# One copy per attention unit moved from VectorE to ScalarE, and sixteen subtractions moved from GpSimd to VectorE, in a float32 decoder layer

## The chip, the core and the metric

The kernel runs on one core of a Trainium2 chip. A core has five engines that run side by side, each through its own instructions in their written order: TensorE (PE in the profile, with its weight loads as PEld), VectorE (DVE), ScalarE (ACT), GpSimd (POOL) and SyncE (SP), which here issues most DMAs. An engine that comes to an instruction whose input is not ready stands still, with everything behind it. The metric is the device time of one execution in microseconds (us).

## The reference, cut to what matters

One decoder layer on 2048 tokens of width 1024, all in float32:

```
mod = silu(c) @ w_ada + b_ada ;  shift, scale, gate = split(mod)
u = x * (1 + scale) + shift
q, k, v, a_gate, p_in, p_gate, m_a, m_p = split(u @ w_in)
a = sliding_window_attention(q, k, v, sinks, bias) * silu(a_gate)  -> @ w_attn_proj
p = causal means of p_in over 2, 4, 8, 16 tokens, minus p_in, by quarter of the width
p = (grouped(p) * pool_scale) * silu(p_gate)                       -> @ w_pool_proj
y = (sigmoid(m_a) * a + sigmoid(m_p) * p) @ w_out * (1 + gate)
out = layer_norm(alpha * x + y)
```

Attention has 16 query heads on 2 key and value heads of 64, a window of 128 tokens, a bias by distance and one extra "sink" logit per head.

## The kernel before, in words

**Exact products from a faster format.** TensorE multiplies in a format that keeps fewer bits than float32 (`F32R`). So each operand is split into a high part (a copy with that type, by ScalarE) and a low part (the operand minus the high part, helper `low`, line 130), and each product is three matmuls: high by high, high by low, low by high (`mm3`). A split of a weight block therefore costs one ScalarE copy and one subtraction, both of 128x512. The split pair stands in a buffer `w_set`, of which there are four.

**Quads.** Dense products are done four at a time. A quad takes two column tiles of weights and two halves of 512 tokens, and gets its four results from seven block products instead of eight, with sums and differences of blocks formed beforehand. The seven are named by their block: T2, B21, T3, B22, B11, T4, T1. Each is 12 matmuls of 128x512 (four slices of the contraction, three matmuls each). The weight sums are made in place in a buffer `W` by GpSimd: `sum1`, then `mid` (two subtractions, which give the blocks of T2 and T3), then `late`. Between the block products VectorE and ScalarE combine accumulators: after T2, for instance, VectorE adds `b = c + p5` (written `mm<-mm,p` in the profile), and T3 may not start before that, since T3 goes on adding into `c`.

**Stages.** The tokens are done in two halves of 1024. Each half has a stage of plain quads (gates, keys, values) and then an attention stage (function `attention`, line 746). After both halves come the output projections and the norm. The change lies inside `attention` alone, which runs twice: from about 270 to 618 us and from about 846 to 1197 us of the profile.

**The attention stage.** It interleaves two streams. The first are 64 units, one per block of 128 queries and pair of heads, and a loop over `n` in which pass `n` works on several units at once. On TensorE a pass is: scores of unit n (`lg<-kk,qs`), transposes of the probabilities of unit n-2 (`pt<-ident,L`), a share of the second stream, and the value product of unit n-2 (`pv<-pth,vv` and `pv<-ptl,vv`). On VectorE: reciprocal of the sums of unit n-1 (`sm`), the treatment of the value product of unit n-3 (line 988 and the two adds behind it), scores plus bias and row maximum (the two `CUSTOM` instructions), the low part of the transposed probabilities (`ptl`), and the scaling of the second head's probabilities (`TENSOR_SCALAR L<-L,sm`). On ScalarE: the scaling of the first head's probabilities (`L<-L,sm`), the high part of the transposed probabilities (`pth`), and two exponentials (`L<-L,nm`).

The value matrix holds high and low part side by side, so a value product comes out as 128 rows: 64 rows from the high part and 64 from the low part. VectorE copies the lower 64 rows from the accumulator to a tile `o2` (`o<-pv`, 64x256) and then adds them to the upper 64 in two adds. This copy is line 988.

The second stream are 13 quads called fills: products for the next steps that fill TensorE's time between a unit's dependent steps. Their order is mix 0, ma 0, q 2, mix 2, ma 2, q 4, mix 4, ma 4, mp 0, q 6, mix 6, ma 6, mp 2, numbered x = 0 to 12. The four "mix" quads end in the pooled branch: GpSimd sums each result over 2, 4, 8 or 16 tokens in doubling steps (`nxt<-vb`, `nxt<-nxt`, `fin<-nxt`), VectorE scales it and subtracts (`fin<-fin,...`), GpSimd multiplies it with its gate (`fin<-fin,pg`). Mix 4 (x = 6) pools over 8 tokens and mix 6 (x = 10) over 16. "q" quads end in the split of queries (`qs`) by ScalarE and VectorE.

The weight split of a block product is written three block products ahead of its use (`split`, line 860): a high part by ScalarE, then a low part by GpSimd, except for the blocks T1, whose low part VectorE makes:

```
            act.copy(hi, q.block(name))
            low(dve if name == "T1" else pool, lo, q.block(name), hi)
            if name == "T1":
                q.mid(pool)
```

So `mid` of a quad stands on GpSimd behind everything written before it, and the high part of T2 on ScalarE waits for `mid`. The order of all these instructions on each engine is the written order; no planner moves them inside the stage.

Of the kernel before, what the change touches and what calls it, by code (L numbers as in the profile page):

```python
# [27 lines left out]
HD = 64  # L28
# [6 lines left out]
POOL_W = (2, 4, 8, 16)  # L35
# [24 lines left out]
def kernel(  # L60
# [23 lines left out]
    pe, act, dve, pool, sp = (Ordered(tc, e) for e in (nc.tensor, nc.scalar, nc.vector, nc.gpsimd, nc.sync))  # L84
# [42 lines left out]
    def as32(ap):  # L127
        return ap.bitcast(F32)

    def low(engine, dst, src, hi):  # L130
        engine.tensor_tensor(dst, src, as32(hi), ALU.subtract)  # L131
# [614 lines left out]
    def attention(ph, s, fills, post, opened):  # L746
# [5 lines left out]
        def ld(name, src, bufs):  # L752
            x = tp.tile([P, CH], F32, tag=name, bufs=bufs, name=name)
            sp.dma_start(x, src)
            return x
# [99 lines left out]
        for i in range(len(seq)):  # L855
            lead = 2 if seq[i] == (K + 1, "B11") else 3
            splits.setdefault(i - lead, []).append(i)
        made, st = {}, {0: [*opened[0][:2], None, None]}

        def split(i):  # L860
            x, name = seq[i]
            q = quads[x]
            if name == "B11" and x > 1:
                q.sum1(pool)
            w = ph.split()
            hi, lo = made[i] = w[:, 0:CH], w[:, CH:]
            act.copy(hi, q.block(name))
            low(dve if name == "T1" else pool, lo, q.block(name), hi)
            if name == "T1":
                q.mid(pool)  # L870
            elif name == "B21":
                q.late(pool)

        def begun(i):
            x, name = seq[i]
            if name == "T1":
                st[x][1] = bank()
                if x < K:
                    later(free_b[0], lambda: seed(x))
                    if free_b[0] < now_n[0]:  # L880
                        run_coming()
            if name == "B11":
                st[x] = [bank(), None, None, None]
                if x < K:
                    quads[x + 1].load(ph, False, sp, None)
            if (x, name) == (K - 1, "B22"):
                quads[K + 1].load(ph, False, sp, None)
            for j in splits.get(i, ()):
                split(j)
# [71 lines left out]
        for i in range(-3, 0):  # L961
            for j in splits.get(i, ()):
                split(j)
# [4 lines left out]
        for n in range(N + 3):  # L968
# [11 lines left out]
            if n - 3 in pvs:  # L980
                pv = pvs.pop(n - 3)
                jj, tt, bb = (n - 3) // U, (n - 3) // NB % 2, (n - 3) % NB
                if bb == 0:
                    outs[jj, tt] = tp.tile([P, CH], F32, tag="o", bufs=2, name="o")
                if bb == 1:
                    ags[jj, tt] = ld("ag", gates_d["ag"][s, jj, tt], 1)
                o2 = tp.tile([HD, 2, P], F32, tag="o2", bufs=1, name="o2")
                dve.tensor_copy(o2, pv[HD:])
                for h in range(2):
                    dve.tensor_tensor(  # L990
                        outs[jj, tt][h * HD : (h + 1) * HD, bb * P : (bb + 1) * P], pv[0:HD, h, :], o2[:, h, :], ALU.add
                    )
# [461 lines left out]
    with Pools("a0") as ph:  # L1454
        opened = attention(ph, 0, plans[0][1], plans[0][2], opened)
# [4 lines left out]
    with Pools("a1") as ph:  # L1460
        opened = attention(ph, 1, plans[1][1], plans[1][2], opened)
# [96 lines left out]
```

## Time and profile before

| what | us |
|---|---|
| median of 3 runs (lowest, highest) | 1728.08 (1727.62, 1729.83) |
| the profiled execution | 1731.03 |
| its span, first to last instruction | 1729.2 |
| busy over the span: PE, DVE, POOL, ACT | 1664.1, 1254.5, 1058.1, 964.2 |
| busy in the first attention stage (348.0): PE, DVE, POOL, ACT | 342.9, 264.2, 260.0, 238.8 |
| busy in the second (351.0): PE, DVE, POOL, ACT | 346.4, 267.3, 259.7, 244.1 |

The profiled execution is 2.95 us slower than the median of the runs, and 1.83 us longer than its span. A row of a timeline reads: start, duration, engine, line, operation, output<-inputs, shape and count, and in brackets the idle time of the engine before it and what ended that wait. Ends of matmuls are modelled, so gaps on TensorE are better read from start to start.

### The profile page before, as it was taken

To read this page: it belongs to the slowest core of one execution; us is meant where nothing else is said; L and a number is where in the kernel's file an instruction comes from. 1 tells how busy PE (TensorE), PEld (TensorE's weight loads), DVE (VectorE), ACT (ScalarE), POOL (GpSimd) and SP (SyncE) were. 2 spreads that over 40 slices of the span, in tenths; PEclk is the share of its full clock that TensorE was granted. 3 is DMA by queue.
4 is the path that set the end of the run, shared out by engine and by line. 5 is a ranking of instruction groups with operands and counts; after the bars stand their busy time and mean duration, and the time that the engine had idled before them with its cause. 6 is when DMAs were issued, how large, how long until landed. Compare 5 with 4: busy or idle time off the path is not lost.

```text
span 1729.2 us, 24722 instructions
## 1 busy us (share of the span) xinstructions
PE 1664.1 (96%) x8056; PEld 1392.5 (81%) x8056; DVE 1254.5 (73%) x2256; ACT 964.2 (56%) x2002; POOL 1058.1 (61%) x782
## 2 busy tenths in 40 slices
PE   6899999999999999999999999999999989999996
PEld 5788888888888788887788888888787767787885
DVE  5966665787778768557578777786778576868877
ACT  4544446667667655334667676765644345434452
POOL 2054427686867837763476778594657875666442
PEclk9999999999999999999999999999999989999999
DMA  9388753333432377866533434235987887787442
GB/s 353 131 283 287 218 188 111 117 108 122 149 107 95 129 250 277 282 226 207 188 110 104 132 118 153 86 116 185 326 294 275 310 305 272 263 274 239 158 139 105
DMA packets 188849, 336.79 MB, mean 195 GB/s; under 512 B 18336, under 2 KB 44080, under 8 KB 188720
## 3 DMA queue, kind: packets, MB, share of 16 engines
q1 hardware_dynamic: 185600, 330.96, 55.7%
q10 hardware_dynamic: 3088, 4.23, 1.0%
q8 instruction: 64, 1.05, 0.3%
q14 instruction: 65, 0.53, 0.1%
q0 software_dynamic: 32, 0.02, 0.0%
HBM read 227.96 MB, written 110.33 MB: 196 GB/s over the span
## 4 chain that ended last, share of the span: by engine, by line
PE 47%; POOL 7%; DVE 5%; DMA 4%; issue 4%; ACT 1%; SPq 0%; POOLq 0%; DVEq 0%; ACTq 0%
PE mm L56 30%; PE lg L56 13%; PE pv L56 2%; PE pt L56 2%; DVE w_set L131 1%; POOL spare L56 1%; POOL nxt L56 1%; POOL W L268 1%; POOL w_set L56 1%; POOL fin L56 1%; DMA W<-in_wpp_dram 1%; DMA W<-in_wap_dram 1%; DMA pin_T<-spare 1%; POOL wide L612 1%; DVE set_T L56 1%
## 5 line engine op out<-in xcount | busy, mean ns | idle before, releaser
L56 PE MATMUL mm<-set_B,w_set 128*128 128x512 f32 x2664 | 664.8, 397 | 18.3 <-ACT w_set L305 10.5
L56 PEld LDWEIGHTS mm<-set_B,w_set 128*128 128x128 f32 x2664 | 501.2, 190 | 129.1 <-ACT w_set L305 12.6
L56 PE MATMUL mm<-set_T,w_set 128*128 128x512 f32 x1824 | 457.4, 397 | 3.8 <-DVE mm L56 1.2
L56 PE MATMUL lg<-set_T,w_set 128*128 128x512 f32 x1728 | 417.9, 392 | 10.0 <-DVE w_set L131 4.8
L56 PEld LDWEIGHTS mm<-set_T,w_set 128*128 128x128 f32 x1824 | 337.7, 189 | 76.4 <-DVE mm L56 4.1
L56 PEld LDWEIGHTS lg<-set_T,w_set 128*128 128x128 f32 x1728 | 323.9, 189 | 82.7 <-DVE w_set L131 8.4
L131 DVE TENSOR_TENSOR w_set<-W,w_set 128x1024 fp32r<-128x1024 f32 x138 | 198.4, 1439 | 185.9 <-ACT w_set L305 172.8
L305 ACT CAST w_set<-W 128x1024 fp32r<-128x1024 f32 x138 | 144.8, 1050 | 291.0 <-PE mm L56 164.4
L56 POOL TENSOR_TENSOR w_set<-W,w_set 128x512 fp32r<-128x512 f32 x132 | 172.0, 1311 | 102.5 <-ACT w_set L56 98.1
L268 POOL TENSOR_TENSOR W<-W,A 128x512 f32<-128x512 f32 x46 | 70.6, 1535 | 223.8 <-DVE set_T L56 58.2
L56 ACT ACTIVATE L<-L,nm 128x257 f32<-128x257 f32 (+1 forms) x256 | 127.1, 498 | 26.0 <-DVE nm L56 20.2
L56 POOL TENSOR_TENSOR W<-W 128x512 f32<-128x512 f32 x82 | 108.3, 1335 | 51.1 <-DVE sm L56 30.3
L277 POOL TENSOR_TENSOR W<-W 128x512 f32<-128x512 f32 x46 | 72.8, 1583 | 101.6 <-DVE w_set L131 94.0
L56 DVE CUSTOM_DVE_ANT_0 L<-lg,bt,nsink 128x256 f32<-128x256 f32 (+1 forms) x256 | 111.6, 473 | 19.0 <-DMA bt<-e_rep 9.1
L56 POOL TENSOR_TENSOR spare<-spare 128x512 f32<-128x512 f32 x68 | 117.2, 1725 | 12.6 <-DMA spare<-ain_B 8.7
L56 ACT CAST w_set<-W 128x512 fp32r<-128x512 f32 (+1 forms) x164 | 100.0, 626 | 37.4 <-POOL W L56 25.8
L56 DVE COPY o<-pv 64x256 f32<-64x256 f32 x128 | 54.3, 424 | 82.7 <-PE pv L56 81.4
L56 ACT CAST pth<-pt 128x512 fp32r<-128x512 f32 (+1 forms) x128 | 72.8, 569 | 62.8 <-PE pt L56 62.4
L56 ACT ACTIVATE L<-L,sm 128x256 f32<-128x256 f32 (+1 forms) x128 | 64.3, 502 | 67.9 <-DVE sm L56 67.7
L272 POOL TENSOR_TENSOR W<-W 128x512 f32<-128x512 f32 x44 | 75.6, 1720 | 39.1 <-DVE w_set L131 30.1
L273 POOL TENSOR_TENSOR W<-W 128x512 f32<-128x512 f32 x44 | 77.5, 1761 | 28.3 <-DMA W<-in_win_dram 26.6
L56 DVE TENSOR_SCALAR L<-L,sm 128x256 f32<-128x256 f32 (+1 forms) x128 | 89.8, 701 | 0.0
(225 smaller groups left out, 2474.8 us busy)
## 6 DMA issues: line engine op xcount, KB each, us to landing
W<-in_win_dram SPq DMA_DIRECT2D x42, 512.0 KB, 5.5
W<-in_win_dram SPq DMA_DIRECT2D x42, 256.0 KB, 3.7
A<-in_win_dram SPq DMA_DIRECT2D x42, 256.0 KB, 4.7
ag_d<-sig SPq DMA_DIRECT2D x32, 256.0 KB, 5.3
pg_d<-sig SPq DMA_DIRECT2D x32, 256.0 KB, 4.4
pg<-pg_d SPq DMA_DIRECT2D x32, 256.0 KB, 3.3
pin_B<-fin SPq DMA_DIRECT2D x32, 256.0 KB, 2.2
ag<-ag_d SPq DMA_DIRECT2D x32, 256.0 KB, 2.9
```

Of the source, the lines that this page charges most:

```text
L56: return lambda *args, **kw: self.tc.keep_in_program_order(op(*args, **kw))
L131: engine.tensor_tensor(dst, src, as32(hi), ALU.subtract)
L268: e.tensor_tensor(self.w[:, 1, :], self.w[:, 2, :], self.a22, ALU.add)
L272: e.tensor_tensor(x[:, 1, :], x[:, 1, :], x[:, 0, :], ALU.subtract)
L273: e.tensor_tensor(x[:, 2, :], x[:, 0, :], x[:, 2, :], ALU.subtract)
L277: e.tensor_tensor(x[:, 3, :], x[:, 3, :], x[:, 1, :], ALU.subtract)
L305: a.copy(by_two(hi), raw)
L612: nc.gpsimd.tensor_tensor(dst, g, dst, ALU.add)
```

## The change

Two edits, both in `attention`. First, the copy of the value product's lower half is issued on ScalarE instead of VectorE; it keeps its place in the pass, ahead of the scaling of the first head's probabilities on ScalarE. That is 64 copies in each stage. Second, a set of pairs (quad, block) names low parts that VectorE makes instead of GpSimd: for the mix quads pooled over 8 and 16 tokens their blocks T3 and T4, and for the quad behind each the blocks T2 and T3. With fills as above that is (6, T3), (6, T4), (7, T2), (7, T3), (10, T3), (10, T4), (11, T2), (11, T3), eight low parts in each stage. The number of instructions in all stays the same.

```diff
         made, st = {}, {0: [*opened[0][:2], None, None]}
+        on_dve = set()
+        for x, (kind, m, _) in enumerate(fills):
+            if kind == "mix" and POOL_W[m // 2] >= 8:
+                on_dve |= {(x, "T3"), (x, "T4"), (x + 1, "T2"), (x + 1, "T3")}
...
             act.copy(hi, q.block(name))
-            low(dve if name == "T1" else pool, lo, q.block(name), hi)
+            low(dve if name == "T1" or (x, name) in on_dve else pool, lo, q.block(name), hi)
...
                 o2 = tp.tile([HD, 2, P], F32, tag="o2", bufs=1, name="o2")
-                dve.tensor_copy(o2, pv[HD:])
+                act.copy(o2, pv[HD:])
```

## The prediction

> **What bounds the kernel now.** I read the page first (TensorE busy 96% of the span, no other engine near it), then the busy time of the two attention stages, then TensorE's waits there, then the timelines around the longest of them. Busy time in the two stages (columns: PE, PEld, DVE, ACT, POOL with counts, granted clock, DMA):
>
> ```profile
> 270.00:618.00 348.00, 342.92 (x1846) 293.46 (x1845) 264.17 (x721) 238.76 (x659) 260.01 (x214) 1.00 0.35 116
> 846.00:1197.00 351.00, 346.43 (x1885) 297.68 (x1886) 267.33 (x721) 244.09 (x661) 259.69 (x206) 1.00 0.36 117
> ```
>
> TensorE bounds both. It is idle for 348.00 - 342.92 = 5.1 us in the first and 4.6 us in the second. No other engine is above 76%. So nothing that the change does to engine totals shows in the time; it can only shorten or lengthen those few waits, and the most that can be won is near 10 us, 0.6%. Averages hide where they are, so next the waits of TensorE in the second stage (us in total, times, longest):
>
> ```profile
> PE pv L56 <- DVE ptl L56: 1.6, 3, 1.1
> ...
> PE mm L56 <- DVE mm L56: 0.9, 2, 0.7
> PE pv L56 <- ACT L L56: 0.7, 1, 0.7
> ```
>
> The 1.1 and the 0.7 are one place, late in the stage. The same place in the first stage, and a place with no wait to compare with (TensorE, start and duration):
>
> ```profile
> 577.41 4.35 PE L56 MATMUL mm<-set_T,w_set 128*128 128x512 f32 x18
> 582.80 0.36 PE L56 MATMUL pv<-pth,vv 128*128 128x256 f32 x1 [1.04 <-ACT L L56]
> 584.25 0.38 PE L56 MATMUL pv<-ptl,vv 128*128 128x256 f32 x1 [1.09 <-DVE ptl L56]
> ...
> 586.16 4.63 PE L56 MATMUL mm<-set_T,w_set 128*128 128x512 f32 x15
> ...
> 1024.20 4.36 PE L56 MATMUL mm<-set_T,w_set 128*128 128x512 f32 x18
> ...
> 1029.69 3.67 PE L56 MATMUL mm<-set_T,w_set 128*128 128x512 f32 x15
> ```
>
> From 18 matmuls to the next group takes 586.16 - 577.41 = 8.75 us here and 1029.69 - 1024.20 = 5.49 us undisturbed: 3.26 us lost. The 15 matmuls that follow take 4.63 instead of 3.67: another 0.96, at a lower clock. Together 4.2 us; the second stage loses 1.1 + 0.7 = 1.8 us at its place. That is 6.0 us, more than half of what can be won. Who is late there, on ScalarE and on GpSimd:
>
> ```profile
> 581.00 0.62 ACT L56 CAST w_set<-W 128x512 fp32r<-128x512 f32 x1 [5.02 <-POOL W L56]
> ```
>
> ```profile
> 572.06 1.74 POOL L56 TENSOR_TENSOR w_set<-A,w_set 128x512 fp32r<-128x512 f32 x1
> ...
> 579.68 2.96 POOL L56 TENSOR_TENSOR W<-W 128x512 f32<-128x512 f32 x2
> ```
>
> ScalarE stands 5.02 us before the high part of T2 of quad 12, which needs the first half of `mid` (579.68). Behind that high part on ScalarE stand the scaling and the `pth` copy that TensorE's value product waits for. GpSimd reaches `mid` late because it works without a pause from the pooled quad 10 on: the 16-token sums of four results, with the low parts of quads 10 and 11 among them. So the end of each stage hangs on GpSimd's backlog.
>
> **The change, part by part.** Prices, from the first stage (busy, mean ns, idle before):
>
> ```profile
> L56 POOL TENSOR_TENSOR w_set<-W,w_set 128x512 fp32r<-128x512 f32 x66 | 85.9, 1310 | 50.6 <-ACT w_set L56 46.2 <-PE mm L56 4.4
> ...
> L56 DVE COPY o<-pv 64x256 f32<-64x256 f32 x64 | 27.1, 424 | 41.1 <-PE pv L56 40.4
> ...
> L56 DVE TENSOR_TENSOR w_set<-W,w_set 128x512 fp32r<-128x512 f32 x14 | 11.4, 812 | 1.4 <-ACT w_set L56 1.2
> ...
> L56 ACT CAST pth<-pt 128x256 fp32r<-128x256 f32 x8 | 2.9, 365 | 4.7 <-PE pt L56 4.7
> ```
>
> *Low parts.* Per stage GpSimd loses 8 x 1.31 = 10.5 us and VectorE gets 8 x 0.81 = 6.5 us. What counts is the backlog at 579.68. Four of the eight belong to quads 6 and 7, long before; the first of quad 10, (10, T3), still falls into a pause. Three, (10, T4), (11, T2) and (11, T3), lie in it: 3 x 1.31 = 3.9 us less work ahead of `mid`. Not all of it is won. Where a VectorE subtraction of this kind meets GpSimd, both stretch:
>
> ```profile
> 571.53 1.11 DVE L56 TENSOR_TENSOR w_set<-W,w_set 128x512 fp32r<-128x512 f32 x1 [0.95 <-ACT w_set L56]
> ```
>
> It takes 1.11 instead of 0.81 on average, and the GpSimd operation at 572.06, which overlaps it, 1.74 instead of 1.31, 0.43 more. So each moved low part relieves GpSimd by 1.31 - 0.43 = 0.88 us at least: 2.6 us for three. `mid` would come at 577.0 or before, the high part at 578.4, `ptl` 2.6 us sooner. TensorE's idle at this place is 1.04 + 1.09 = 2.1 us, so 2.6 covers it; the lower clock behind it goes as well. I take the whole 4.2 + 1.8 = 6.0 us. Bounds: 0 and 6.0. What is late next there: ScalarE still waits some 2 us for `mid`, with 0.5 us to spare for TensorE.
>
> The Trainium skill says under "SBUF — State Buffer", section "Who interferes with whom", that a VectorE instruction with two SBUF inputs holds the port that it shares with GpSimd for its whole length, so that a GpSimd instruction that reads SBUF is blocked until it ends. That speaks against this part, and the stretched pair agrees in kind (0.43 of 1.11 us); what it would make of the time is the second rival.
>
> *The copy.* 64 per stage leave VectorE (0.42 each) and go to ScalarE. The trace has no such copy on ScalarE; the nearest row is `pth` with 256 columns from the same kind of memory, 0.37 us. In a usual pass both engines stand idle when the value product ends (VectorE waits 40.4 us in all before this copy), and on ScalarE the copy plus the scaling fit into the time until the transposes are done; the adds follow at the same time as before, within 0.1 us. So nothing in a usual pass. It differs where one of the two is late. Where VectorE is late it saves 0.42 us, and `ptl` behind it comes sooner, as here (TensorE):
>
> ```profile
> 357.17 0.28 PE L56 MATMUL pv<-pth,vv 128*128 128x256 f32 x1
> 357.58 0.38 PE L56 MATMUL pv<-ptl,vv 128*128 128x256 f32 x1
> ```
>
> The second value matmul follows 0.41 us behind the first instead of 0.12: 0.3 us that go. In the second stage such waits on `ptl` are 1.6 - 1.1 = 0.5 us. Gain 0.8 us, bounds 0 and 0.8.
>
> Where ScalarE is late it costs. The place that I can see best is quad 10 (VectorE, ScalarE, TensorE):
>
> ```profile
> 534.33 0.43 DVE L56 COPY o<-pv 64x256 f32<-64x256 f32 x1
> ...
> 537.79 0.69 DVE L56 TENSOR_TENSOR mm<-mm,p 128x512 f32<-128x512 f32 x1
> ```
>
> ```profile
> 534.47 0.62 ACT L56 CAST w_set<-W 128x512 fp32r<-128x512 f32 x1
> ```
>
> ```profile
> 538.53 0.96 PE L56 MATMUL mm<-set_T,w_set 128*128 128x512 f32 x3 [0.78 <-DVE sm L56]
> ```
>
> VectorE's add `b = c + p5` ends at 537.79 + 0.69 = 538.48, and T3 starts at 538.53: the add, which stands behind the whole unit on VectorE, is what T3 waits for. On ScalarE the copy would start after the high part at 534.47, at 535.09, and end at 535.46, against 534.76 before: 0.7 us later, and T3 with it. One such place per stage: 1.4 us. In quad 11, where (11, T3) is put ahead of such a unit on VectorE and T3 is just as close (the `mm <- DVE mm` waits above), VectorE is later by 0.81 - 0.42 = 0.4 us: 0.8 us for two stages. The other moved low parts fall on passes where VectorE idles or has over 1 us in hand; without that cover each would cost up to 0.81 us. Cost 2.2 us; bounds 0, and the first rival's 16.0.
>
> *Sum.* -6.0 - 0.8 + 2.2 = -4.6 us against the profiled execution's 1731.03, so 1726.4; that execution is 2.95 above the median of the runs, and 1728.08 - 4.6 = **1723.5 us**. No other stage gets another instruction.
>
> **The rivals.**
>
> *ScalarE's lateness reaches TensorE (slower).* Copies that ScalarE would reach late, the first and the last of them (VectorE's copy, and the ScalarE instruction ahead of the new one):
>
> ```profile
> 285.57 0.42 DVE L56 COPY o<-pv 64x256 f32<-64x256 f32 x1 [0.15 <-PE pv L56]
> ...
> 1163.97 0.43 DVE L56 COPY o<-pv 64x256 f32<-64x256 f32 x1
> ```
>
> ```profile
> 286.15 0.62 ACT L56 CAST w_set<-W 128x512 fp32r<-128x512 f32 x1 [0.60 <-POOL W L56]
> ...
> 1164.37 0.62 ACT L56 CAST w_set<-W 128x512 fp32r<-128x512 f32 x1
> ```
>
> At the first the copy would end at 286.77 + 0.4 instead of 285.99, 1.2 us later. Of the 128 copies 23 would end later, by 0.06 to 1.9 us, 16.0 us in all, and VectorE's adds, score maxima and `ptl` wait behind each. If all of it landed: 1728.08 - 6.8 + 0.8 + 16.0 = 1738.1. It decides from 9.5 of the 16.0 on (59%), where the kernel is slower by 0.2%. For it: ScalarE becomes a link between value product and scores in every unit. Against it: TensorE idles under 5.1 us in a stage with these units in it, so it hardly feels VectorE's and ScalarE's lateness as it is, and some of it goes with the backlog (1164.37 stands behind the late `mid`).
>
> *The low parts hold GpSimd up as long as they run.* Then each relieves GpSimd by 1.31 - 0.81 = 0.5 us, three by 1.5; 2.1 - 1.5 = 0.6 us of idle stays in the first stage, 0.3 in the second, and half of the 0.96 at a lower clock. Gain 6.0 - 1.4 = 4.6 in place of 6.0: 1724.9.
>
> *The backlog is not what holds the end.* If `mid` waits for something else as long, the 6.0 do not come, and 1728.08 - 0.8 + 2.2 = 1729.5. Against it: GpSimd has no pause before it.
>
> *More goes.* If nearly all idle time and the lower clock go, 5.1 + 4.6 + 0.96 = 10.7 us: 1717.4. Against it: the waits at the opening of the first stage are untouched.
>
> **How the numbers follow.** Chances: my forecast (1721 to 1724.6) 0.42; held-up GpSimd (1724.6 to 1726) 0.18; backlog not the cause (1726 to 1731) 0.16; more goes (below 1721) 0.12; ScalarE's lateness (above 1731) 0.12. A measurement can tell about 0.2%, 3.5 us, from no change, so faster means below 1724.6: 0.42 + 0.12 + 0.04 of the second case = 0.58; slower 0.12; same 0.30. The range 1717 to 1730.5 leaves out half of the "more" case's lower end and the slow case. The likeliest case's own range is 1721 to 1724.6.
>
> **What the profile after would show.** Right: no 5 us wait of ScalarE for `mid` near the end of either stage, no value product there with a wait on `ptl`, the clock full, the stage after some 3 us sooner in each half. T3 of quads 10 and 11 waits 0.4 to 0.7 us longer for the add. Wrong: if new waits on `ptl` or on the add stand all over the stage, the first rival holds; if ScalarE still waits 5 us, the third.

## The result and the profile after

The changed kernel takes 1723.83 us (median of 11 runs, 1722.12 to 1727.65) against 1728.33 us for the kernel before in the same comparison (11 runs): a ratio of 0.9976, 95% interval 0.9968 to 0.9985 (the two medians alone give 0.9974). That is 0.24% or 4.1 us, with an interval of 2.6 to 5.5 us, just beyond what the measurement can tell from no change. Forecast was 4.6 us. The time came out right; several terms of the sum did not, and they cancelled. Ratios are of fast executions alone; one execution of 6595.8 us, of the kernel with the copy and the low parts of quads 6 and 7, is not in its ratio.

First the page of the profile of the changed kernel, busy time by engine:

```profile
PE 1657.4 (96%) x8056; PEld 1387.5 (81%) x8056; DVE 1200.8 (70%) x2144; ACT 1012.6 (59%) x2130; POOL 1047.2 (61%) x766
```

VectorE lost 53.7 us of busy time, ScalarE gained 48.4 and GpSimd lost 10.9, about half of the 16 x 1.31 = 21 us of low parts that left it. None of that is the gain, as none of them was the bound. What a copy and a low part take now (groups of the changed kernel, first the ScalarE one, then two of VectorE):

```profile
L56 ACT COPY o<-pv 64x256 f32<-64x256 f32 x128 | 47.4, 370 | 74.8 <-PE pv L56 73.4
```

```profile
L56 DVE TENSOR_SCALAR L<-L,sm 128x256 f32<-128x256 f32 x120 | 74.1, 618 | 0.0
...
L56 DVE TENSOR_TENSOR w_set<-W,w_set 128x512 fp32r<-128x512 f32 x40 | 33.9, 847 | 11.3 <-ACT w_set L56 10.9
```

The copy costs ScalarE 0.370 us (0.37 was taken), a low part VectorE 0.847 (0.81 was taken; the 40 are the 28 that VectorE made before and 12 of the 16 moved ones). The scaling of the second head's probabilities, which nobody moved, became shorter; more on that below.

The end of the first attention stage (timeline of TensorE, changed kernel; start, duration, and in brackets the wait), and the same place in the second:

```profile
575.84 4.35 PE L56 MATMUL mm<-set_T,w_set 128*128 128x512 f32 x18
...
581.45 0.39 PE L56 MATMUL pv<-ptl,vv 128*128 128x256 f32 x1 [0.74 <-DVE ptl L56]
...
582.88 3.66 PE L56 MATMUL mm<-set_T,w_set 128*128 128x512 f32 x15
```

```profile
1152.98 4.35 PE L56 MATMUL mm<-set_T,w_set 128*128 128x512 f32 x18
...
1157.91 0.39 PE L56 MATMUL pv<-ptl,vv 128*128 128x256 f32 x1 [0.46 <-DVE ptl L56]
...
1159.37 3.70 PE L56 MATMUL mm<-set_T,w_set 128*128 128x512 f32 x15
```

The second place as it was before (timeline of TensorE, kernel before):

```profile
1156.38 4.35 PE L56 MATMUL mm<-set_T,w_set 128*128 128x512 f32 x18
...
1164.22 3.70 PE L56 MATMUL mm<-set_T,w_set 128*128 128x512 f32 x15
```

From the 18 matmuls to the 15 takes 582.88 - 575.84 = 7.04 us in the first stage, 8.75 before: 1.71 less. The 15 take 3.66, at the full clock, 4.63 before: 0.97 less. In the second stage it is 6.39 instead of 7.84: 1.45 less. So the two ends gave 4.1 us, not 6.0, and undisturbed (5.49) there would be another 1.55 and 0.90.

Part of the 4.1 is the clock. Before, the granted clock behind the first stall was 0.51 for 3.4 us (stretch, its length, busy time and count of PE, PEld, DVE, ACT and POOL, granted clock, DMA):

```profile
584.80:588.20 3.40, 3.40 (x14) 3.01 (x13) 3.29 (x11) 3.37 (x10) 3.32 (x4) 0.51 0.51 189
```

Besides the 0.97 it cost some 0.5 us ahead of the 15 matmuls: from the end of the wait for `ptl` to the 15 it took 586.16 - 584.25 = 1.91 us, and 582.88 - 581.45 = 1.43 in the changed kernel. A stall of that size does not always bring such a stretch: the second end before waited 1.7 us in all and kept the clock, and with the copy alone (below) the first end kept it (waits of 1.39 and 0.74 us) and the second lost it (1.05 and 0.74 us, clock 0.50 from 1165.7 to 1169.1). So 1.4 of the 4.1 us belong to one execution, and how often they arise is not known.

What still holds the ends (ScalarE, GpSimd and VectorE of the changed kernel):

```profile
578.23 0.62 ACT L56 CAST w_set<-W 128x512 fp32r<-128x512 f32 x1 [3.94 <-POOL W L56]
```

```profile
570.54 1.75 POOL L56 TENSOR_TENSOR fin<-fin,pg 128x512 f32<-128x512 f32 x1
...
576.89 3.00 POOL L56 TENSOR_TENSOR W<-W 128x512 f32<-128x512 f32 x2
```

```profile
576.97 1.76 DVE L56 SCALAR_TENSOR_TENSOR fin<-fin,p 128x512 f32<-128x512 f32 x1 [3.52 <-POOL fin L56]
...
579.27 0.58 DVE L56 TENSOR_TENSOR o<-pv,o 64x128 f32<-64x128 f32 x2 [0.46 <-ACT o L56]
```

VectorE before, for comparison:

```profile
579.75 1.76 DVE L56 SCALAR_TENSOR_TENSOR fin<-fin,p 128x512 f32<-128x512 f32 x1 [3.52 <-POOL fin L56]
```

`mid` starts at 576.89 instead of 579.68, and ScalarE still waits 3.94 us for it. TensorE now waits for `ptl` alone, and two things make `ptl` late. VectorE stands 3.52 us before the scaling of the last pooled result, just as long as before, and runs it beside `mid` in 1.76 us. Then it stands another 0.46 us for the copy, which is on ScalarE now, behind the high part that waits for `mid`. So the wait that ends last is still the one for `mid`; the last pooled result is 0.46 us ahead of it.

Where the change cost (TensorE, both kernels, the stretches of quads 6 to 8; only the rows that waited). Before, in the second stage:

```profile
1018.08 0.39 PE L56 MATMUL pv<-ptl,vv 128*128 128x256 f32 x1 [0.19 <-DVE ptl L56]
...
1038.18 1.65 PE L56 MATMUL mm<-set_T,w_set 128*128 128x512 f32 x6 [0.69 <-DVE mm L56]
```

Changed kernel, first the first stage (where the kernel before had no wait in this stretch), then the second:

```profile
439.54 0.38 PE L56 MATMUL pv<-ptl,vv 128*128 128x256 f32 x1 [0.34 <-DVE ptl L56]
...
459.00 1.66 PE L56 MATMUL mm<-set_T,w_set 128*128 128x512 f32 x6 [0.48 <-DVE mm L56]
...
1013.63 0.38 PE L56 MATMUL pv<-pth,vv 128*128 128x256 f32 x1 [0.37 <-ACT pth L56]
1014.49 0.39 PE L56 MATMUL pv<-ptl,vv 128*128 128x256 f32 x1 [0.47 <-DVE ptl L56]
...
1034.89 1.66 PE L56 MATMUL mm<-set_T,w_set 128*128 128x512 f32 x6 [1.03 <-DVE mm L56]
```

These waits sum to 2.69 us, 0.88 before: 1.8 us more, where the prediction had put nothing.

### The profile page after: what moved, and what is told of

Its sections match the earlier page's. It is cut to its first block, busy times and chain, and to the rows that moved or that the text cites. A ratio compares the mean times of both kernels' runs of the same rounds, so it can differ in the third digit from the quotient of the medians.

```text
span 1721.7 us, 24720 instructions
## 1 busy us (share of the span) xinstructions
PE 1657.4 (96%) x8056; PEld 1387.5 (81%) x8056; DVE 1200.8 (70%) x2144; ACT 1012.6 (59%) x2130; POOL 1047.2 (61%) x766
## 3 DMA queue, kind: packets, MB, share of 16 engines
q8 instruction: 64, 1.05, 0.3%
## 4 chain that ended last, share of the span: by engine, by line
PE 74%; DVE 9%; POOL 5%; DMA 5%; issue 4%; ACT 3%; SPq 0%; POOLq 0%; DVEq 0%; ACTq 0%
PE mm L56 48%; PE lg L56 19%; PE pv L56 4%; PE pt L56 4%; DVE w_set L131 2%; POOL W L268 1%; DVE set_T L56 1%; POOL wide L612 1%; POOL spare L56 1%; DMA g<-mp_d 1%; DMA g<-ma_d 1%; ACT w_set L305 1%; POOL W L273 1%; POOL W L272 1%; DVE qs L56 1%
## 5 line engine op out<-in xcount | busy, mean ns | idle before, releaser
L56 PE MATMUL mm<-set_B,w_set 128*128 128x512 f32 x2664 | 661.4, 395 | 18.5 <-ACT w_set L305 10.9
L56 POOL TENSOR_TENSOR w_set<-W,w_set 128x512 fp32r<-128x512 f32 x120 | 157.1, 1317 | 115.0 <-ACT w_set L56 113.0
L56 DVE TENSOR_TENSOR o<-pv,o 64x128 f32<-64x128 f32 x256 | 72.0, 281 | 133.5 <-ACT o L56 127.2
L56 ACT COPY o<-pv 64x256 f32<-64x256 f32 x128 | 47.4, 370 | 74.8 <-PE pv L56 73.4
L56 DVE TENSOR_TENSOR ptl<-pt,pth 128x512 fp32r<-128x512 f32 (+1 forms) x128 | 85.7, 669 | 1.3 <-ACT pth L56 1.0
```

The costliest lines, as they stand in the source:

```text
L56: return lambda *args, **kw: self.tc.keep_in_program_order(op(*args, **kw))
```

## The experiments

Each ratio is to the kernel before, on the same chip. The next column is the length of both attention stages together in the profiled execution, from the start of the first `pth` copy to the start of the last in each: 329.95 + 331.12 = 661.07 us before. The last two are what TensorE loses in the last eighth of each stage: the time from the start of one matmul to the next, beyond what this pair of shapes takes undisturbed at the full clock, summed over losses above 0.1 us. Inside the stages only two of these traces have a stretch of half clock: the kernel before, in its first stage (1.4 us of its 661.07 and of its 4.20), and the copy alone, in its second (some 1.5 us of its 3.87). Apart from that single executions repeat well: the 28th `ptl` of the first stage starts 138.85 to 138.89 us behind the first in all nine kernels with one copy on ScalarE, and 139.19 or 139.20 in the four without.

| kernel | ratio (95%) | both stages, us | end of first, second, us |
|---|---|---|---|
| before | 1 | 661.07 | 4.20, 2.25 |
| changed kernel | 0.9976 (0.9968, 0.9985) | -3.55 | 1.40, 0.85 |
| copy alone | 0.9998 (0.9987, 1.0008) | -0.34 | 2.66, 3.87 |
| eight low parts alone | 1.0001 (0.9990, 1.0011) | +0.61 | 1.67, 1.44 |
| copy, low parts of quads 10 and 11 | 0.9960 (0.9948, 0.9973) | -5.12 | 1.12, 0.85 |
| changed kernel, copy twice | 1.0046 (1.0032, 1.0059) | +8.00 | 2.49, 0.48 |
| before without gate products of quad 10 | 0.9954 (0.9941, 0.9966) | -7.83 | none, none |
| copy, three low parts | 0.9963 (0.9951, 0.9975) | -6.41 | 1.22, 0.83 |
| the same, last `mid` on VectorE | 0.9959 (0.9945, 0.9972) | -6.47 | 1.33, 0.77 |
| low parts of quads 10 and 11, no copy | 0.9985 (0.9976, 0.9994) | -3.38 | 1.43, 1.43 |
| copy, three low parts, gate products on VectorE | 0.9967 (0.9955, 0.9978) | -4.04 | none, none |
| copy, low parts of quads 6 and 7 | 0.9999 (0.9989, 1.0009) | +0.63 | 2.66, 2.29 |
| copy, gate products on VectorE | 0.9969 (0.9956, 0.9981) | -4.77 | 1.79, 1.53 |
| copy, three low parts, third gate product on VectorE | 0.9940 (0.9926, 0.9953) | -6.93 | 0.66, 0.34 |

**Each part alone.** The copy alone:

```diff
-                dve.tensor_copy(o2, pv[HD:])
+                act.copy(o2, pv[HD:])
```

> The copy on ScalarE alone; all low parts as before. Theory (GpSimd's backlog holds the end of both stages): the long waits at the end of the stages stay, 5 us of ScalarE before quad 12's T2; the copy saves under 1 us where VectorE is late and costs 1 to 2 us where ScalarE is late, so 1727.5 to 1730, ratio 0.9995 to 1.001. Rival (VectorE's relief from 128 copies is the gain): most of the 4.5 us comes with this edit alone, ratio 0.998 or less. Second rival (ScalarE's lateness reaches TensorE): slower by 3 us and more.

The low parts alone, the copy left on VectorE:

```diff
+        on_dve = set()
+        for x, (kind, m, _) in enumerate(fills):
+            if kind == "mix" and POOL_W[m // 2] >= 8:
+                on_dve |= {(x, "T3"), (x, "T4"), (x + 1, "T2"), (x + 1, "T3")}
...
-            low(dve if name == "T1" else pool, lo, q.block(name), hi)
+            low(dve if name == "T1" or (x, name) in on_dve else pool, lo, q.block(name), hi)
```

> The sixteen low parts on VectorE alone; the copy stays on VectorE. Theory: the end of the stages gains its 6 to 7 us, and VectorE, which is not relieved of the copies, gives back some 0.8 us at each place where TensorE waits for its add (quads 7, 10 and 11): ratio about 0.998 to 0.999, a bit slower than both edits together. Rival (VectorE's relief is the gain): slower than before, ratio 1.001 or more, since VectorE only gets work.

Neither gives anything by itself: 0.9998 and 1.0001; for the low parts 0.998 to 0.999 had been expected, and that did not come (0.9990 to 1.0011). With the copy alone the end stays (TensorE at the end of the first stage, then ScalarE there):

```profile
585.13 0.38 PE L56 MATMUL pv<-pth,vv 128*128 128x256 f32 x1 [1.39 <-ACT pth L56]
586.26 0.39 PE L56 MATMUL pv<-ptl,vv 128*128 128x256 f32 x1 [0.74 <-DVE ptl L56]
```

```profile
583.04 0.62 ACT L56 CAST w_set<-W 128x512 fp32r<-128x512 f32 x1 [5.20 <-POOL W L56]
```

The 5 us wait for `mid` is still there, so the copy has no part in curing it. But ahead of the ends the copy gains: from the first `pth` copy to the 18 matmuls this kernel is 1.03 us sooner than before in the first stage and 0.30 in the second. The low parts alone cut the end, and their cost eats it elsewhere (waits of TensorE in the first stage: total, times, longest; low parts alone, then the changed kernel):

```profile
PE pv L56 <- DVE ptl L56: 3.0, 4, 1.1
```

```profile
PE pv L56 <- DVE ptl L56: 1.1, 2, 0.7
```

With the copy gone from VectorE, waits for `ptl` fall from 3.0 to 1.1 us. The two edits are not two gains that add up: the low parts give the gain, and the copy pays for what they cost VectorE.

**Which low parts.** Only those of the quad pooled over 16 tokens and the one behind it, with the copy and without:

```diff
-            if kind == "mix" and POOL_W[m // 2] >= 8:
+            if kind == "mix" and POOL_W[m // 2] >= 16:
```

> Both edits, but low parts moved only for the quad pooled over 16 tokens and the one behind it (quads 10 and 11); quads 6 and 7 keep theirs on GpSimd. Theory: quads 6 and 7 lie 140 us ahead of the end, so the end gains as much as with the whole change, and the 1 to 2 us that the trace of after lost around quads 6 and 7 come back: ratio 0.9965 to 0.9975. Rival (each moved low part brings its share): half of the gain is lost, ratio about 0.999.

> Four low parts per stage (quads 10 and 11) on VectorE, none for quads 6 and 7, and the copy left on VectorE. Theory: the low parts alone lost as much around quads 6 and 7 as they won at the end, so without those two quads most of the gain shows without the copy: ratio 0.997 to 0.998. Rival (the gain needs VectorE to be relieved of the copies): ratio 0.9995 to 1.0005.

Half of the low parts do better than all: 1.57 us shorter over both stages than the changed kernel (the intervals of the two ratios overlap a little). Taking the copy back costs 0.9985 - 0.9960 = 0.25%, some 4 us, and 1.74 us of stage length. Its 0.9985 lies between the theory and the rival of that run, so the low parts of quads 10 and 11 are worth something without the copy, but less than with it. Then the other half, those of quads 6 and 7 alone with the copy:

```diff
-            if kind == "mix" and POOL_W[m // 2] >= 8:
+            if kind == "mix" and POOL_W[m // 2] == 8:
```

> The copy on ScalarE, and only the four low parts of quads 6 and 7 in each stage on VectorE. Theory: these four lie in passes where GpSimd catches up again before the end, so they bring nothing there (end stall 2.7 and 3.9 us, as with the copy alone) and cost 1 to 2 us in quads 6 to 8: ratio 0.9995 to 1.0015. Rival: GpSimd's backlog at the end is carried over from quads 6 and 7; then the end stall is cut by a third or more, and the ratio is below 0.9985.

They bring nothing (0.9999): the stages are 0.97 us longer than with the copy alone. GpSimd's backlog is not carried over from quads 6 and 7: the first end has 2.66 in both, and at the second the difference (2.29 against 3.87) is the half clock of the kernel with the copy alone. Its waits there are 1.05 and 0.74 us, here 1.01 and 0.74.

Then the three low parts that the prediction said matter:

```diff
+                on_dve |= {(x, "T4"), (x + 1, "T2"), (x + 1, "T3")}
```

> The copy on ScalarE and only three low parts per stage on VectorE: T4 of quad 10, T2 and T3 of quad 11, those that lie in GpSimd's stretch without a pause. Theory: the end gains as with four low parts, and the wait of T3 of quad 10 for the add gets shorter by up to 0.4 us per stage, since (10, T3) no longer stands ahead of it on VectorE: ratio 0.9955 to 0.9962, 0 to 1 us faster than with four. Rival (every moved low part brings its share): a quarter of the gain is lost, ratio 0.997.

Three low parts a stage do all that eight do, and by stage length more: -6.41 us over both stages (the ratios' intervals overlap). Leaving (10, T3) on GpSimd is worth 6.41 - 5.12 = 1.3 us of it.

**How much the backlog is worth.** The kernel before, with GpSimd's multiplication of the pooled result with its gate left out in quad 10:

```diff
-                pool.tensor_tensor(p, p, pg, ALU.mult)
+                if POOL_W[m // 2] < 16:
+                    pool.tensor_tensor(p, p, pg, ALU.mult)
```

> The kernel before, with nothing moved, but without GpSimd's multiplication by the pool gate for the results of the quad pooled over 16 tokens (four per stage, three of them ahead of the late weight sums of quad 12). So part of the computation is left out; GpSimd's backlog is 3.9 us shorter and no other engine gets work. Theory (the backlog holds the end of both stages): the end of the stages gains 5 to 7 us and nothing is lost in the middle: ratio 0.996 to 0.997. Rival (the end is held by something else, by VectorE for instance): ratio 0.999 to 1.0.

TensorE has no wait at the end (first stage, TensorE and ScalarE):

```profile
576.76 4.36 PE L56 MATMUL mm<-set_T,w_set 128*128 128x512 f32 x18
...
582.28 3.68 PE L56 MATMUL mm<-set_T,w_set 128*128 128x512 f32 x15
```

```profile
577.59 0.62 ACT L56 CAST w_set<-W 128x512 fp32r<-128x512 f32 x1 [2.49 <-POOL W L56]
```

5.52 us from group to group, 5.49 undisturbed, with no work added to any engine: 0.9954, and 7.83 us over both stages. So GpSimd's backlog is the cause, and what it costs the two stages in all (6.4 without the 1.4 of the clock) is more than the 6.0 that the prediction had for their ends. How much of that is VectorE's work running with less of GpSimd's beside it was not separated.

**What the copy costs ScalarE.** The changed kernel with the copy issued twice:

```diff
                 act.copy(o2, pv[HD:])
+                act.copy(o2, pv[HD:])
```

> The whole change with the ScalarE copy of the value product's lower half issued twice, 128 more copies of some 0.37 us (47 us of ScalarE). If ScalarE's lateness reaches TensorE everywhere, the time grows by 10 us and more over the whole change (ratio to before above 1.003). Theory: most passes have cover, and only the few places where TensorE waits for VectorE's add or for the transposed probabilities pay, some ten per stage at up to 0.4 us: 2 to 6 us more than the whole change, ratio 0.9985 to 1.001.

It became 0.7% slower than the changed kernel (1.0046 against 0.9976), some 12 us for 128 x 0.37 = 47 us of ScalarE: a quarter comes through. That is the sign that had been set for ScalarE's lateness reaching TensorE (10 us and more, above 1.003), and not the theory's 2 to 6 us: with a second copy that rival holds. The first copy fits into ScalarE's pauses, the second doesn't. Of the 12 us, 4.4 are TensorE's waits for VectorE's adds, 2.7 us in the whole span of the changed kernel and here:

```profile
PE mm L56 <- DVE mm L56: 7.1, 7, 2.0
```

**What is left at the end.** First theory: `mid` on GpSimd is still late. With the three low parts, the last `mid` on VectorE:

```diff
-                q.mid(pool)
+                q.mid(dve if x == K - 1 else pool)
```

> As the three low parts, and the two subtractions of quad 12's weight sums (mid) on VectorE as well, which idles over 3 us there waiting for GpSimd. Theory: the high part of T2 of quad 12 no longer waits for GpSimd at all, and the 1.1 and 0.85 us that TensorE still loses at the end of the stages go: another 1 to 2 us, ratio 0.9945 to 0.9955. Rival (behind the weight sums the value product waits for VectorE, which waits for GpSimd's pooled sums): no further gain, ratio as with the three low parts.

The ratio stayed (0.9959 against 0.9963), and so did the loss of 1.33 and 0.77, but it lies one pass earlier (VectorE, then TensorE, first stage):

```profile
571.21 3.14 DVE L56 TENSOR_TENSOR W<-W 128x512 f32<-128x512 f32 x2
```

```profile
575.48 0.39 PE L56 MATMUL pv<-pth,vv 128*128 128x256 f32 x1 [0.44 <-DVE nm L56]
576.23 0.39 PE L56 MATMUL pv<-ptl,vv 128*128 128x256 f32 x1 [0.36 <-DVE ptl L56]
...
577.29 4.36 PE L56 MATMUL mm<-set_T,w_set 128*128 128x512 f32 x18
...
582.79 3.67 PE L56 MATMUL mm<-set_T,w_set 128*128 128x512 f32 x15
```

`mid` takes VectorE 3.14 us, and the value product of that pass waits for what stands behind it. From the 18 to the 15 matmuls it is 5.50 us, undisturbed, but TensorE comes there 1.2 us later than with the three low parts alone. So there was no gain, and whether `mid` on GpSimd alone held the end this run cannot say. Second theory: what VectorE waits for is the sum `fin`, which stands on GpSimd behind the gate product of the pooled result before it (1.75 us at 570.54 in the changed kernel). With the gate products of quad 10 on VectorE, with and without the three low parts:

```diff
-                pool.tensor_tensor(p, p, pg, ALU.mult)
+                (dve if POOL_W[m // 2] >= 16 else pool).tensor_tensor(p, p, pg, ALU.mult)
```

> The copy on ScalarE, the three low parts (10, T4), (11, T2), (11, T3) on VectorE, and in the quads pooled over 16 tokens also the multiplication with the pool gate on VectorE. Theory: what is left of the end stall (1.22 and 0.83 us start to start with the three low parts) is VectorE's wait of 3.5 us for a pooled sum that stands on GpSimd behind such a multiplication of 1.75 us; without it the wait is under 2 us, the value product does not wait for ptl, and both stages together end another 1 to 2 us sooner than with the three low parts alone (7 to 8.5 us sooner than before): ratio to before 0.9945 to 0.996. Rival: VectorE's own load is what is left; four more operations of about 0.7 us in each stage make it later, the end stall stays or grows, and the ratio is 0.997 or more.

> The copy on ScalarE, no low part moved, and the multiplication with the pool gate on VectorE in the quads pooled over 16 tokens (four in each stage, about 1.3 to 1.75 us each on GpSimd). Theory: the end of the stage hangs on GpSimd's backlog, whatever it consists of; 5 us or more less work ahead of mid cures it as three low parts (3.9 us) do: end stall under 1.3 us in both stages, ratio 0.995 to 0.997. Rival: the low parts matter because high parts on ScalarE and block products stand right behind them; then the end stall stays above 2 us, ratio 0.998 or more.

With the low parts the end stall went, as this theory had it, but the ratio did not follow: 0.9967. The time is lost a quad earlier (VectorE, then TensorE, first stage):

```profile
561.00 1.68 DVE L56 TENSOR_TENSOR fin<-fin,pg 128x512 f32<-128x512 f32 x1
```

```profile
566.06 0.96 PE L56 MATMUL mm<-set_T,w_set 128*128 128x512 f32 x3 [1.81 <-DVE mm L56]
```

The second gate product stands on VectorE ahead of the add that T3 of quad 11 waits for. Without any low part the gate products do about what the three low parts do by the ratio (0.9969), with 1.6 us less gain in stage length and a rest at the end (1.79 and 1.53) between the theory's (under 1.3) and the rival's (above 2). So work of another kind ahead of `mid` on GpSimd counts too, not the low parts as such. Last, only the third gate product:

```diff
+                third = POOL_W[m // 2] >= 16 and (m % 2, t) == (1, 0)
-                pool.tensor_tensor(p, p, pg, ALU.mult)
+                (dve if third else pool).tensor_tensor(p, p, pg, ALU.mult)
```

> The three low parts and the copy, and of the four pooled results of quad 10 only the third is multiplied with its gate by VectorE. Theory: with all four on VectorE the end stall went, but the second multiplication (1.68 us) stood ahead of the add that T3 of quad 11 waits for, 2.5 and 2.4 us lost; the third falls into a stretch of 2.4 us in which VectorE waits for ScalarE's copy and costs nothing, and it takes away the 1.75 us that hold the last pooled sum and mid on GpSimd. So no end stall (under 0.3 us in either stage, against 1.22 and 0.83), no new one in quad 11, both stages together 8 to 8.8 us shorter than before, ratio 0.994 to 0.9958. Rival: VectorE's load at the end is what is left, however it is put: an end or quad 11 stall of over 1 us in each stage, ratio 0.9963 or more.

The third gate product and the last pooled result (VectorE, first stage, this kernel):

```profile
563.53 0.72 DVE L56 TENSOR_TENSOR fin<-fin,pg 128x512 f32<-128x512 f32 x1
...
575.55 1.76 DVE L56 SCALAR_TENSOR_TENSOR fin<-fin,p 128x512 f32<-128x512 f32 x1 [2.39 <-POOL fin L56]
```

VectorE does it in 0.72 us in a pause, and its wait for the last pooled sum falls from 3.52 to 2.39 us. The end is down to 0.66 and 0.34, quad 11 has no new stall, and the ratio is 0.9940 (0.9926, 0.9953): the fastest of all, and clearly faster than the changed kernel. The rest of the end was to be under 0.3 us and the stages 8 to 8.8 us shorter; they are 6.93. Over the three low parts alone that is 0.5 us of stage length, and the two intervals just touch, so what the third gate product adds to them is not settled. The ratio's interval is 8.1 to 12.8 us, more than the stages' 6.93; what lies outside the stages is not explained.

## Why the prediction was right, and which of its steps were not

**That the ends hang on GpSimd's backlog: right.** Without the gate products the end stall is gone (0.9954), and work taken from GpSimd ahead of `mid` takes away a good part of it: of 4.20 + 2.25 = 6.45 us, 1.4 of them the clock's, 2.05 are left with the three low parts and 3.32 with the gate products on VectorE. The rival that the backlog is not the cause is out.

**That all 6.0 us go: too much; 4.1 went at the two places.** The step that failed is "`mid` would come at 577.0 or before ... 2.6 covers it". `mid` did come at 576.89. But TensorE was there 1.57 us sooner too (575.84 against 577.41), so against TensorE `mid` gained only 2.79 - 1.57 = 1.2 us. I had set the relief against a TensorE that stands still. What is late next is the high part on ScalarE, as I had it, but without the 0.5 us to spare: by the copy behind it `ptl` is 0.74 us late, with the last pooled result close ahead. The second place I had sized by its waits, 1.8 us; from start to start it lost 7.84 - 5.49 = 2.35, and 1.45 of that went. The rival of the held-up GpSimd had 0.6 and 0.3 us of idle left, nearer to the 0.74 and 0.46 us waits found. It had them by another way, and half of the lower clock left besides; in the profiled execution that went altogether.

**That each stage ends some 3 us sooner: in the first only.** The first is 3.31 us shorter, 1.4 of it the clock's, the second 0.24.

**That only three of the eight matter: right.** The three alone do no worse than the eight, and better by stage length.

**That the low parts of quads 6 and 7 cost nothing: wrong, and the largest miss of sign.** The step is "fall on passes where VectorE idles or has over 1 us in hand". They cost 1.57 us over the stages (changed kernel against quads 10 and 11 alone) and the waits rose by 1.8 us. VectorE's low parts now have 11.3 us of idle time in front of them (40 of them, the row at the top; 2.6 for the 28 before), nearly all of it for high parts from ScalarE. So the moved subtraction brings a wait into the pass along with its 0.85 us, and what stands behind it on VectorE, `ptl` and the adds, comes later by both. How much each of the two makes was not separated.

**That T3 of quad 10 comes 0.7 us later in each stage: the place right, the mechanism wrong.** VectorE, GpSimd and TensorE there, before:

```profile
536.87 0.99 DVE L56 TENSOR_SCALAR L<-L,sm 128x256 f32<-128x256 f32 x1
```

```profile
536.42 1.30 POOL L56 TENSOR_TENSOR o<-o,ag 128x512 f32<-128x512 f32 x1
```

```profile
529.48 4.38 PE L56 MATMUL mm<-set_T,w_set 128*128 128x512 f32 x18
...
534.76 2.99 PE L56 MATMUL mm<-set_B,w_set 128*128 128x512 f32 x12
```

and in the changed kernel:

```profile
536.86 0.34 DVE L56 TENSOR_SCALAR L<-L,sm 128x256 f32<-128x256 f32 x1
```

```profile
535.74 1.29 POOL L56 TENSOR_TENSOR o<-o,ag 128x512 f32<-128x512 f32 x1
```

```profile
528.52 4.38 PE L56 MATMUL mm<-set_T,w_set 128*128 128x512 f32 x18
...
534.06 3.02 PE L56 MATMUL mm<-set_B,w_set 128*128 128x512 f32 x12
537.86 0.96 PE L56 MATMUL mm<-set_T,w_set 128*128 128x512 f32 x3 [0.78 <-DVE mm L56]
```

Against the group of 12 matmuls VectorE's adds of the value product start 0.77 us in (534.83), not 0.08 (534.84 before): 0.7 us later, as worked out. But T3 starts 3.80 us in, and 3.77 before. The 0.7 us came back in the scaling behind them: before, it started while GpSimd's multiplication (536.42 to 537.72) ran and ended just after it; now GpSimd is nearly done when it comes, and it takes 0.34 instead of 0.99 us. From the 18 matmuls of T2's group to T3 it is 537.86 - 528.52 = 9.34 us, and 538.53 - 529.48 = 9.05 before, so 0.3 us was lost, where 0.7 had been forecast, and nearly all of it ahead of the 12 matmuls (534.06 - 528.52 = 5.54 us, 5.28 before), not at the add. In the second stage it is 9.24 us, 8.82 before: 0.4 lost. With the copy and the three low parts, (10, T3) left on GpSimd, it is 8.79 us in the first (TensorE) and 8.69 in the second:

```profile
528.72 4.38 PE L56 MATMUL mm<-set_T,w_set 128*128 128x512 f32 x18
...
537.51 0.96 PE L56 MATMUL mm<-set_T,w_set 128*128 128x512 f32 x3 [0.52 <-DVE mm L56]
```

So (10, T3) costs 0.55 us in each stage here, and the copy, which was to cost 0.7, costs nothing: without (10, T3) the place is 0.26 and 0.13 us shorter than before.

**That T3 of quad 11 comes 0.4 us later: wrong.** TensorE at that place in the first stage, before and then in the changed kernel:

```profile
561.95 2.88 PE L56 MATMUL mm<-set_B,w_set 128*128 128x512 f32 x12
565.12 1.28 PE L56 MATMUL mm<-set_T,w_set 128*128 128x512 f32 x3 [0.29 <-DVE mm L56]
```

```profile
561.28 2.88 PE L56 MATMUL mm<-set_B,w_set 128*128 128x512 f32 x12
564.00 0.84 PE L56 MATMUL mm<-set_T,w_set 128*128 128x512 f32 x3
```

It started 3.17 us behind the group of 12, and now 2.72, without a wait: 0.45 us sooner, and 0.2 sooner in the second stage. VectorE comes to its add 0.9 us sooner against the group of 12: 0.4 of it ahead of the adds of the value product, where the copy stood, and 0.46 in the scaling behind them, which takes 0.80 us instead of 1.26.

**That late places of VectorE give 0.8 us: at least that.** The one that was shown, the 0.41 us between two value matmuls at 357, went. With the copy alone TensorE is 1.03 + 0.30 = 1.3 us sooner by the 18 matmuls of the two ends, costs included. Over the whole stages it is 0.34: behind the ends it loses again, as below.

**The rival of ScalarE's lateness: did not come with one copy, and came with two.** One copy is free or better in all; a second costs a quarter of its length. My reason against it, that TensorE hardly feels ScalarE's lateness, holds for the first 24 us a stage and not for the next 24.

So the sum of -4.6 met the measured -4.1 in part by luck. In the profiled executions the two ends gave 4.1 us, not 6.0, and 1.4 of it is a stretch of half clock. Ahead of the ends, from the first `pth` copy of a stage to the 18 matmuls, the changed kernel is 1.04 us sooner in the first stage and 0.81 us later in the second: 0.2 us sooner in all, where the forecast had -0.8 + 2.2, 1.4 us later. It got there by other steps, which the kernels of the experiments give one after the other, taken at the same place: the copy gains 1.3 us, the three low parts another 1.7, (10, T3) costs 1.2 and the low parts of quads 6 and 7 cost 1.6. Behind the ends 0.4 us a stage are lost at the last units, in every kernel with the copy on ScalarE and in none without: the copy now stands ahead of the last `pth`, a cost that the prediction had put at nothing. -4.1 - 0.2 + 0.8 = -3.5, the stage length of the table.

That the 4.1 us of the ratio equal the 4.1 us of the ends is chance. Without the clock's 1.4 the stages are only 2.1 us shorter, below the ratio's interval of 2.6 to 5.5. The mean granted clock of the 11 executions of the changed kernel is 0.9913, that of the 65 executions of the kernel before beside the experiments 0.9900, so part of the gain may be less time at half clock. Nor does the clock settle it alone: the low parts alone have 0.9911 and gain nothing. This was not separated.

## What to carry to other kernels

Where an engine works off a backlog, find the few operations that stand between the backlog's start and the one that is waited for, and move only those: here three of eight gave the whole gain, and by stage length the other five took some of it back. A move of work onto an engine whose order is fixed is priced by what stands behind it in that pass, not by that engine's idle share; if it must be moved, take something off the same engine, since here neither edit was worth anything alone. And set each relief against where the waiting engine will then be, as it comes sooner too.

## What the runs showed of the hardware that I had not expected

A VectorE scaling of 128x256 takes 0.34 us in one place and 0.99 in another, by what GpSimd is doing as it starts: in quad 10 it ended 0.14 us after the GpSimd multiplication that was under way. In the trace before, 40 of the 120 have no GpSimd operation beside them and take 0.34 to 0.35 us each; the other 80 take 0.89 on average, and 0.77 in the changed kernel (77 of them). So an instruction that comes later can end at the same time, and part of a delay on VectorE disappears there. Over the whole kernel the mean of this scaling went from 710 ns to 618 (rows of the groups, before and after):

```profile
L56 DVE TENSOR_SCALAR L<-L,sm 128x256 f32<-128x256 f32 x120 | 85.2, 710 | 0.0
```

That is 11 us of VectorE time that no edit touched. The Trainium skill says under "SBUF — State Buffer", section "Who interferes with whom", that a VectorE operation in a mode with two ports, which a scaling of this kind can enter, contends with GpSimd: whoever issues first has the shared pair of ports for the whole instruction, and the other is blocked. The trace agrees in kind, and not quite in size: blocked until GpSimd's end at 537.72 and then working 0.34 us, the scaling would end at 538.06, and it ended at 537.86.
